# Two token-major sections of 512 columns in a diffusion block, with the attention's values read back from DRAM

## The chip, the cores and the metric

The kernel runs on one core of a Trainium2 chip, all in one launch. The metric is the device time in microseconds (us). The program is built with a tile framework: the source names operations on tiles, and the framework inserts the waits and sets the order in which each engine issues its instructions, following its own estimate of when each is ready. The engines are PE (TensorE, matmuls), DVE (VectorE), ACT (ScalarE), POOL (GpSimd) and SP (SyncE, which issues most DMAs). Each engine works through its own queue in order.

## The reference

One layer of a hybrid backbone is applied to 512 sample tokens and 128 context tokens (640 rows, `T`; the samples are `TS` = 512 of them). What matters here:

```python
proj = h @ lw['w_in']                     # (640, 1024) @ (1024, 3328)
(a_x, a_b, a_c, b_q, b_ff, b_fb, b_i, b_g, c_q, c_k, c_v, d_u, d_v) = split(proj)   # 256 columns each
y_b, s_f, s_b = hgrn2_bidir(b_q, b_ff, b_fb, b_i, b_g, ...)
#   o = o_f + o_b;  o = o * rsqrt(mean(o * o, per head) + EPS);  y_b = o * norm_g * silu(b_g)
y_c = neighbourhood_attention(qh, kh, vh, ctx_k, ctx_v, rpb)    # samples: 8x16 windows on an 8 x 64 grid
#     context_attention(qh, kh, vh)                              # context tokens
y_d = chunk_gmlp(d_u, d_v, ...)            # rmsnorm of d_v over its 256 columns, then a product with d_u
merged = sum of gate_x * (y_x @ w_br_x) over the four branches;  return merged @ w_o
```

The rest (adaLN modulation, a convolutional FFN of 2 x 2816 columns, norms) follows or surrounds it. The context's keys and values are outputs too.

## The kernel before

**Stages.** A boot stage normalizes the input and makes its transposed copy, split into a high and a low part in a rounded 32-bit type (`xh`, `xl`), as every weight is. A product of two such operands is three matmuls: high x high, low activation x high weight, high activation x low weight. Then come the 13 sections of `w_in`, the gates and branches, `w_o`, and the FFN.

**Units.** The work is a list of units, each with a load, a preparation (`wsplit`: ACT makes the high part, DVE the low one) and a compute step. Loads are issued up to four units ahead, preparations two ahead; raw weights have three buffers, prepared ones three. Sections are listed in `SECTIONS` (L57): ff, fb, q, i, g, dv, du, ck, cq, cv, ac, ax, ab, with two units each. For the sections in `LOWD` (ac, ax, ab, and gate d) the low part is made by a DMA that adds into its target, issued from POOL.

**Two layouts.** Most sections are feature-major (`in_tile`, L904): a 128 x 128 block of the weight is stationary, 320 tokens move, twice per block, and the result has features on partitions. The sections i and dv are token-major (`tok_tile`, L917): a block of `xh` or `xl` with 128 tokens is stationary, 256 weight columns move, and the result has tokens on partitions. Such a section holds five PSUM banks over its two units: both `g` buffers (two banks each) and one of the four `m` banks. ACT empties them (L939) at its end.

**Jobs beside it.** HGRN (`hgrn`, from L448), gMLP (`gmlp`), the short convolution, the attention (`attn`) and the adaLN columns (`ada_cols`) are Python generators. `tick` adds the estimated PE time of each step of a unit, and runs a job's next piece when its due time has come. So small matmuls of the jobs stand between the large ones of the units. A dictionary `R` tells one job of another's progress.

**HGRN's end** (L614 to L658). Once the gate is there (`g_done`), five token tiles of the output are made in PSUM; ACT copies them to `og` (L631) and squares them (L632), DVE reduces and scales (L611). Then each tile is transposed (L649) and multiplied by the gate, which is feature-major like the result (L653). The whole is split into high and low parts (`split_y`, L663 and L664) and stored to DRAM (`ybd`).

**Attention's values.** cv is feature-major in region G. The attention needs its values token-major, in seven windows of 128 tokens (two rows of blocks of 8 x 8 grid cells) in `vw`, and the context's values in `vpt`. It makes them by PE transposes of `cv` (L750, L763), copied out of PSUM by DVE (L754, L765). The first reader of `vpt` is the context attention (L800), that of `vw` the first piece of the window attention (L866).

**Regions.** Large buffers are shared by name (`region`): the next tile of a region waits until the last reader of the one before is done.

## Time and profile before

| | us |
|---|---|
| median of 3 runs | 1022.59 (1022.56 to 1022.63) |
| span of the profiled execution | 1020.8 |
| PE busy in the span | 1008.7 (99%) |
| DVE busy | 789.7 (77%) |
| ACT busy | 538.4 (53%) |
| POOL busy | 106.1 (10%) |

The profiled execution's own time is its span, 1020.8 us, and some 1.8 us around it make up the time of a run. The touched part lies between about 64 and 285 us of the span. In rows of the timeline the columns are start, duration (both us), engine, line, operation, output<-inputs, shape and count; what ended the engine's idle time before stands in brackets. A row with a count merges neighbours of the same kind. Groups of instructions read: line, engine, operation, tiles, shape, count | busy us, mean ns of one | idle time before. Matmuls overlap in the records, so a matmul's duration is longer than the time until the next one starts.

### The profile page before, as it was taken

Reading aid. Unit: us, or ns where it says so; the run is one execution under the profiler, and the core shown is the slowest. Engines: PE = TensorE matmul, PEld = TensorE weight load, DVE = VectorE, ACT = ScalarE, POOL = GpSimd, SP = SyncE. Lnnn points to the kernel's source line nnn. Section 1 sums busy time; section 2 is a strip of 40 time slices with the busy share of each in tenths; the row PEclk is TensorE's granted clock in tenths of the full one; section 3 lists DMA queues with packets and bytes.
Section 4 is the critical chain, followed back from the end, with each engine's and each line's share of the span. In section 5 each row is a group of like instructions: output and inputs, shape, how many; then the busy total and the mean of one; then the engine's idle time right before and its main releaser. Section 6 shows DMA issues by size and latency. Waiting matters only on the chain.

```text
span 1020.8 us, 18766 instructions
## 1 busy us (share of the span) xinstructions
PE 1008.7 (99%) x7572; PEld 953.0 (93%) x7572; DVE 789.7 (77%) x1308; ACT 538.4 (53%) x933; POOL 106.1 (10%) x153
## 2 busy tenths in 40 slices
PE   8999999999999999999999999999999999999997
PEld 6899999999999999999998899999999999888886
DVE  6759899779857676776868879988888887797644
ACT  6642343354545454444544567777777776633432
POOL 1000020322100000000010111111122211001101
PEclk9999999999999999999999999999999999999999
DMA  9864333697562413323288585755555669974212
GB/s 355 322 217 130 126 117 116 168 284 226 120 207 79 155 58 104 136 66 104 61 283 337 212 325 121 198 151 150 150 151 151 157 161 274 363 249 157 83 42 103
DMA packets 55926, 177.85 MB, mean 174 GB/s; under 512 B 8192, under 2 KB 14624, under 8 KB 53280
## 3 DMA queue, kind: packets, MB, share of 16 engines
q1 hardware_dynamic: 45008, 140.60, 40.2%
q0 software_dynamic: 10832, 36.06, 14.7%
q8 instruction: 59, 0.97, 0.4%
q14 instruction: 27, 0.22, 0.1%
HBM read 134.93 MB, written 25.46 MB: 157 GB/s over the span
## 4 chain that ended last, share of the span: by engine, by line
PE 92%; DVE 4%; DMA 2%; ACT 1%; issue 1%; SPq 0%; POOLq 0%; POOL 0%; DVEq 0%; ACTq 0%
PE g L1480 20%; PE m L1124 17%; PE g L363 14%; PE g L1815 8%; PE m L1815 6%; PE g L1137 5%; PE m L1480 4%; PE m L1264 3%; PE g L935 2%; PE g L1264 2%; PE m L149 2%; PE g L149 1%; PE m L1475 1%; PE m L527 1%; DMA A<-in_w_ada_dram 1%
## 5 line engine op out<-in xcount | busy, mean ns | idle before, releaser
L363 PE MATMUL g<-XH,w 128*128 128x320 f32 x704 | 171.0, 317 | 0.1
L363 PEld LDWEIGHTS g<-XH,w 128*128 128x128 f32 x704 | 120.6, 188 | 2.5 <-issue 1.0
L363 PE MATMUL g<-XL,w 128*128 128x320 f32 x352 | 108.7, 309 | 0.0
L363 PEld LDWEIGHTS g<-XL,w 128*128 128x128 f32 x352 | 66.3, 188 | 0.1
L312 DVE TENSOR_TENSOR w<-raw,w 128x1024 fp32r<-128x1024 f32 x34 | 41.5, 1221 | 14.7 <-ACT w L311 9.0
L1124 PE MATMUL m<-XH,w 128*128 128x320 f32 x224 | 52.5, 309 | 0.0
L1815 PE MATMUL g<-w,XH 128*128 128x512 f32 (+1 forms) x216 | 50.2, 385 | 0.0
L1815 PEld LDWEIGHTS g<-w,XH 128*128 128x128 f32 x216 | 39.5, 188 | 8.3 <-ACT XH L1774 0.3
L311 ACT ACTIVATE w<-raw 128x1024 fp32r<-128x1024 f32 x34 | 35.7, 1049 | 21.4 <-PE g L1264 9.9
L1815 PE MATMUL g<-w,XL 128*128 128x512 f32 (+1 forms) x180 | 42.5, 387 | 0.0
L149 DVE SCALAR_TENSOR_TENSOR X<-MG,p2t,X 128x641 f32<-128x641 f32 x44 | 38.9, 884 | 4.3 <-ACT X L149 3.4
L149 DVE SCALAR_TENSOR_TENSOR X<-X,p2t,X 128x641 f32<-128x641 f32 x44 | 38.8, 883 | 1.9 <-ACT X L149 1.0
L1815 PEld LDWEIGHTS g<-w,XL 128*128 128x128 f32 x180 | 33.4, 188 | 7.4 <-DVE dt L1830 0.7
L149 ACT ACTIVATE w<-raw 128x1024 fp32r<-128x1024 f32 (+3 forms) x46 | 38.5, 852 | 2.5 <-DMA raw<-in_w_in_dram 1.4
L1480 PE MATMUL g<-XL,w 128*128 128x320 f32 x240 | 38.6, 310 | 0.0
L1480 PE MATMUL g<-XL,C 128*128 128x320 f32 x240 | 38.4, 309 | 0.0
L1124 PEld LDWEIGHTS m<-XH,w 128*128 128x128 f32 x224 | 38.2, 188 | 0.0
L1480 PEld LDWEIGHTS g<-XL,w 128*128 128x128 f32 x240 | 36.0, 188 | 0.5 <-ACT MG L149 0.3
L1815 PE MATMUL m<-w,XH 128*128 128x512 f32 (+1 forms) x156 | 36.4, 381 | 0.0
L1480 PEld LDWEIGHTS g<-XL,C 128*128 128x128 f32 x240 | 36.0, 188 | 0.4 <-ACT MG L149 0.4
L1124 PE MATMUL m<-XL,w 128*128 128x320 f32 x112 | 34.6, 309 | 0.0
L1815 PEld LDWEIGHTS m<-w,XH 128*128 128x128 f32 x156 | 28.5, 188 | 5.6
(549 smaller groups left out, 2749.8 us busy)
## 6 DMA issues: line engine op xcount, KB each, us to landing
raw<-in_w_up_dram SPq DMA_DIRECT2D x30, 512.0 KB, 5.0
raw<-in_w_gp_dram SPq DMA_DIRECT2D x21, 640.0 KB, 3.9
raw<-in_w_down_dram SPq DMA_DIRECT2D x22, 512.0 KB, 4.2
raw<-in_w_in_dram SPq DMA_DIRECT2D x19, 512.0 KB, 4.3
H<-in_w_adt_dram SPq DMA_DIRECT2D x16, 512.0 KB, 4.2
actd<-X POOLq DMA_DIRECT2D x22, 320.5 KB, 5.5
X<-in_w_adt_dram SPq DMA_DIRECT2D x10, 512.0 KB, 4.3
upd<-XL SPq DMA_DIRECT2D x4, 1280.0 KB, 6.5
```

Of the source, the lines that this page charges most:

```text
L149: r = f(*args, **kw)
L311: act(w[0], raw, AF.Copy)
L312: vec.tensor_tensor(w[1], raw, w[0].bitcast(F32), ALU.subtract)
L363: mm(o, w[:, h, k0 + k, :], r(k)[:, s], start=(k == 0 and i == 0), stop=(k == kt - 1 and i == 2))
L527: mm(m[W * g:W * g + W, (i - s0) * W:(i - s0 + 1) * W], lhs, rhs, start=True, stop=True, tile_position=(64 * par, W * g))
L935: mm(o, x(kx)[:, ts], w[:, h, k, :], start=(kx == 0 and i == 0), stop=(kx == 7 and i == 2))
L1124: mm(o, w[:, k, :], x[:, k, :], start=(first and k == 0 and j == 0), stop=(k == 3 and j == 2), skip_group_check=True)
L1137: mm(pb[:, c, 0:HC], w[:, h + k, :], y[:, x, k, s], start=(k == 0 and j == 0), stop=(k == 1 and j == 2))
L1264: mm(m, mh[k // 2][:, hx, k % 2, t * P:(t + 1) * P], wo[q][:, hw, k % 2, :], start=(k == 0 and i == 0), stop=(k == 7 and i == 2))
L1475: mm(o, w[:, k, :], x[:, k, :], start=(first and not part and k == 0 and j == 0), stop=(part == 1 and k == 3), skip_group_check=True)
L1480: z = mm(o, w[:, k, :], x[:, k, :], start=(first and k == 0 and j == 0), stop=(k == 3 and j == 2), skip_group_check=True)
L1815: mm(ps, sl[k][hx][:, t * P:(t + 1) * P], w[:, hw, k, c0:c1], start=first, stop=end and (last or nh == 1 and t == 4 and kk_ == 7))
```

## The change

The four sections i, dv, g and cv become two token-major sections of 512 columns: `iv` holds i and dv, `gc` holds g and cv. Each has four units, each unit two of the eight k blocks with 512 columns. Their weights are packed on the host accordingly; the loads keep their size of 512 KB. The order of the sections changes: du follows iv directly, gc follows du.

The gate is token-major now. HGRN multiplies it in while it takes the output from PSUM, on DVE; after the transposes, ACT and DVE write the high and low parts piece by piece straight from PSUM, and `split_y` is not called there.

The attention's values are token-major too. ACT copies each token tile of cv from PSUM into a small buffer (tag `gt`, shared with other short-lived tiles), and SP stores it to a DRAM tile `cvd`. The attention job loads `vpt` with one DMA and each of the seven windows with two DMAs of 64 partitions. The transposes and their copies are gone, and region G is not used for cv. The attention and `g_operands` start after cq, which has the place that cv had.

```diff
--- before.py
+++ after.py
@@ -54,7 +54,8 @@
 
 OFF = dict(ax=0, ab=256, ac=512, q=768, ff=1024, fb=1280, i=1536, g=1792,
            cq=2048, ck=2304, cv=2560, du=2816, dv=3072)
-SECTIONS = ["ff", "fb", "q", "i", "g", "dv", "du", "ck", "cq", "cv", "ac", "ax", "ab"]
+SECTIONS = ["ff", "fb", "q", "iv", "du", "gc", "ck", "cq", "ac", "ax", "ab"]
+TOK = {"iv": ("i", "dv"), "gc": ("g", "cv")}
 
 
 C_C, C_BADA, C_N1, C_N2 = 0, 16, 64, 72
@@ -405,9 +406,6 @@
         elif sec == "q":
             dd = need("D", "HD", [P, 2560])
             act(c2(dd[:, n * T:(n + 1) * T]), psv, AF.Silu)
-        elif sec == "g":
-            o = need("MG1", "HO", [P, 2560])
-            act(c2(o[:, 1280 + n * T:1280 + (n + 1) * T]), psv, AF.Silu)
         elif sec == "du":
             x0 = need("X0", "DX0", [P, 2560])
             act(c2(x0[:, n * T:(n + 1) * T]), psv, AF.Copy)
@@ -425,13 +423,10 @@
             if (sec, n) == ("ab", 1):
                 drain(lambda: "ada39" in R)
                 R["ya"] = split_y("A", y[:, 1].rearrange("p n t -> p (n t)"))
-        elif sec in ("ck", "cq", "cv"):
-            if sec == "cv":
-                dst = need("G", "CG", [P, 1280])[:, n * T:(n + 1) * T]
-            else:
-                f = need("F", "CF", [P, 2560])
-                o = 0 if sec == "ck" else 1280
-                dst = f[:, o + n * T:o + (n + 1) * T]
+        elif sec in ("ck", "cq"):
+            f = need("F", "CF", [P, 2560])
+            o = 0 if sec == "ck" else 1280
+            dst = f[:, o + n * T:o + (n + 1) * T]
             sc = 0.125 if sec == "cq" else 1.0
             cg, cw = (4, 16) if sec == "cq" else (8, 8)
             dv = dst[:, 0:TS].rearrange("p (g r c) -> p r g c", g=cg, r=8)
@@ -441,6 +436,7 @@
             act(dst[:, TS:T], ps[:, 1, 192:320], AF.Copy, scale=sc)
 
 
+    cvd = dram.tile([T, 256], F32, name="cvd")
     ybd, ycd = [dram.tile([P, 2, 2, T], F32, name=n) for n in ("ybd", "ycd")]
 
 
@@ -628,8 +624,9 @@
                        vt[:, t * 256 + h * 64:t * 256 + (h + 1) * 64],
                        start=(t == 4), stop=(t == 4 or par == 1), skip_group_check=True)
                     pe(0.21)
-            act(og[:, t * 256:(t + 1) * 256], m[:, 0:256], AF.Copy)
-            act(o2[:, t * 256:(t + 1) * 256], m[:, 0:256], AF.Square)
+            tb = slice(t * 256, (t + 1) * 256)
+            act(o2[:, tb], m[:, 0:256], AF.Square)
+            vec.tensor_tensor(og[:, tb], m[:, 0:256], sg[:, tb], ALU.mult)
             yield 0.5
 
             s4 = ss[:, 4 * t:4 * t + 4]
@@ -643,17 +640,19 @@
         normed(last)
         R["hgrn_y"] = True
         yield HY
+        w = region("D", [P, 2, 2, T], F32R)
         for t in range(5):
             m = pm()
             for pr in range(2):
                 ten.transpose(m[:, pr * P:(pr + 1) * P],
                                     og[:, t * 256 + pr * P:t * 256 + (pr + 1) * P], ident)
                 pe(0.11)
-                s = sg[:, pr * T + t * P:pr * T + (t + 1) * P]
-                vec.scalar_tensor_tensor(s, m[:, pr * P:(pr + 1) * P],
-                                         p1[:, C_HN + pr:C_HN + pr + 1], s, ALU.mult, ALU.mult)
+                h, l = [w[:, x, pr, t * P:(t + 1) * P] for x in range(2)]
+                mo, gn = m[:, pr * P:(pr + 1) * P], p1[:, C_HN + pr:C_HN + pr + 1]
+                act(h, mo, AF.Copy, scale=gn)
+                vec.scalar_tensor_tensor(l, mo, gn, h.bitcast(F32), ALU.mult, ALU.subtract)
             yield 0.4
-        nc.sync.dma_start(ybd, split_y("D", sg).bitcast(F32))
+        nc.sync.dma_start(ybd, w.bitcast(F32))
         R["hgrn_done"] = True
         R["yd"] = split_y("E", R["yt"])
 
@@ -717,7 +716,6 @@
         while "yd" not in R:
             yield 1
         ck, cq = R["CF"][:, 0:1280], R["CF"][:, 1280:2560]
-        cv = R["CG"]
         x0 = region("X0", [P, 2560])
         x1 = region("X1", [P, 2560])
         bm = region("B", [P, 2560])
@@ -742,27 +740,16 @@
         pool.memset(btt[:, :, 256:384], 0.0)
 
         offs = [0, 2, 4, 6, 1, 3, 5]
-        for g in range(0, 7, 2):
-            grp = offs[g:g + 2]
-            m = pm()
-            for j, o in enumerate(grp):
-                for pr in range(2):
-                    ten.transpose(m[:, (j * 2 + pr) * P:(j * 2 + pr + 1) * P],
-                                        cv[:, pr * T + o * 64:pr * T + o * 64 + P], ident)
-                pe(0.22)
-            n_ = len(grp) * 256
-            vec.tensor_copy(vw[:, g * 256:g * 256 + n_], m[:, 0:n_])
-            yield 0.4
+        nc.sync.dma_start(vpt, cvd[TS:T])
+        cvw = cvd[0:TS].rearrange("(r g c) v -> r g c v", r=8, c=8)
+        for i, o in enumerate(offs):
+            for g in range(2):
+                nc.sync.dma_start(vw[64 * g:64 * g + 64, i * 256:(i + 1) * 256], cvw[:, o + g])
         m = pm()
         for pr in range(2):
             ten.transpose(m[:, pr * P:(pr + 1) * P], ck[:, pr * T + TS:(pr + 1) * T], ident)
             pe(0.11)
         vec.tensor_copy(ktk, m[:, 0:256])
-        m = pm()
-        for pr in range(2):
-            ten.transpose(m[:, pr * P:(pr + 1) * P], cv[:, pr * T + TS:(pr + 1) * T], ident)
-            pe(0.11)
-        vec.tensor_copy(vpt, m[:, 0:256])
         R["cg"] = True
         nc.sync.dma_start(o_cv[0, 0].rearrange("h s d -> s h d"), vpt.rearrange("p (h d) -> p h d", h=4))
         yield 0.4
@@ -898,8 +885,8 @@
     def plain(ld, cp):
         units.append((ld, lambda pr: pr(), cp))
 
-    SLACK = {"q": 1.3, "du": 1.4, "ax": 1.0, "cv": 1.1}
-    starts = {"q": hgrn, "du": gmlp, "ax": conva, "cv": attn}
+    SLACK = {"q": 1.3, "du": 1.4, "ax": 1.0, "cq": 1.1}
+    starts = {"q": hgrn, "du": gmlp, "ax": conva, "cq": attn}
 
     def in_tile(sec, n, w):
         ps = pg()
@@ -909,49 +896,55 @@
             R[sec + "_done"] = True
         if n == 1 and sec in starts:
             start(starts[sec](), 1.5, SLACK[sec])
-            if sec == "cv":
+            if sec == "cq":
                 start(g_operands())
             if sec == "q":
                 start(ada_cols(range(16, 40), "S0", col_home, HD[4], 10), HD[7])
 
-    def tok_tile(sec, kh, w):
-
-        if kh == 0:
+    def tok_tile(sec, kq, w):
+
+        if kq == 0:
             g0, g1 = pg(), pg()
-            R[sec + "_ps"] = [g0[:, 0, :], g0[:, 1, :], g1[:, 0, :], g1[:, 1, :], pm()]
-            if sec == "i":
-                dst = need("E", "HE", [P, 2560])[:, 1280:2560]
+            R["tok_ps"] = [g0[:, 0, :], g0[:, 1, :], g1[:, 0, :], g1[:, 1, :], pm()]
+            if sec == "iv":
+                need("E", "HE", [P, 2560])
+                R["DX1"] = region("X1", [P, 2560])
             else:
-                dst = region("X1", [P, 2560])
-                R["DX1"] = dst
-            R[sec + "_dst"] = dst
-        dst = R[sec + "_dst"]
+                need("MG1", "HO", [P, 2560])
         for t in range(5):
-            o = R[sec + "_ps"][t][:, 0:256]
-            for k in range(4):
-                ts = slice(t * P, (t + 1) * P)
-                kx = kh * 4 + k
+            o = R["tok_ps"][t]
+            ts = slice(t * P, (t + 1) * P)
+            for k in range(2):
+                kx = kq * 2 + k
                 for i, (x, h) in enumerate(((xhk, 0), (xlk, 0), (xhk, 1))):
                     mm(o, x(kx)[:, ts], w[:, h, k, :], start=(kx == 0 and i == 0), stop=(kx == 7 and i == 2))
-                tick(0.33)
-            if kh == 1:
-                v = dst[:, t * 256:(t + 1) * 256]
-                act(v, o, AF.Copy)
-                if sec == "dv":
-                    act(dst[:, 1280 + t * 256:1280 + (t + 1) * 256], v, AF.Square,
-                        accum_out=dss[:, t:t + 1])
-        if kh == 1:
-            R[sec + "_done"] = True
-
-    TOK = ["i", "dv"]
+                tick(0.68)
+            if kq < 3:
+                continue
+            cs = slice(t * 256, (t + 1) * 256)
+            if sec == "iv":
+                vi, dv = R["HE"][:, 1280:2560], R["DX1"]
+                act(vi[:, cs], o[:, 0:256], AF.Copy)
+                act(dv[:, cs], o[:, 256:512], AF.Copy)
+                act(dv[:, 1280 + t * 256:1280 + (t + 1) * 256], dv[:, cs], AF.Square, accum_out=dss[:, t:t + 1])
+            else:
+                act(R["HO"][:, 1280 + t * 256:1280 + (t + 1) * 256], o[:, 0:256], AF.Silu)
+                c = gp.tile([P, 256], F32, tag="gt", name=nm("cv"))
+                act(c, o[:, 256:512], AF.Copy)
+                nc.sync.dma_start(cvd[ts], c)
+        if kq == 3:
+            R["i_done" if sec == "iv" else "g_done"] = True
+
     for s in SECTIONS:
+        if s in TOK:
+            i = list(TOK).index(s)
+            for kq in range(4):
+                plain(lambda i=i, kq=kq: rows(a["w_tok"][i, kq], 2, 512),
+                      lambda w, s=s, kq=kq: tok_tile(s, kq, w))
+            continue
         for n in range(2):
-            if s in TOK:
-                plain(lambda s=s, n=n: rows(a["w_tok"][TOK.index(s), n], 4, 256),
-                      lambda w, s=s, n=n: tok_tile(s, n, w))
-            else:
-                plain(lambda s=s, n=n: feat(a["w_in"][OFF[s] // P + n], dma=s in LOWD),
-                      lambda w, s=s, n=n: in_tile(s, n, w))
+            plain(lambda s=s, n=n: feat(a["w_in"][OFF[s] // P + n], dma=s in LOWD),
+                  lambda w, s=s, n=n: in_tile(s, n, w))
 
     hdr = dram.tile([2, 2, P, 4, HC], F32, name="hdr")
 
@@ -2139,8 +2132,8 @@
 
     w_in = f("w_in")[0]
     arr["w_in"] = tiles(w_in, 8, P)
-    arr["w_tok"] = np.stack([tiles(w_in[:, OFF[s]:OFF[s] + 256], 8, 256)[0].reshape(P, 2, 4, 256)
-                             .transpose(1, 0, 2, 3) for s in ("i", "dv")])
+    w = [np.concatenate([w_in[:, OFF[s]:OFF[s] + 256] for s in x], 1) for x in TOK.values()]
+    arr["w_tok"] = np.stack([tiles(x, 8, 512)[0].reshape(P, 4, 2, 512).transpose(1, 0, 2, 3) for x in w])
     br = np.concatenate([f("w_br_" + b)[0] for b in "abcd"], 1)
     arr["w_gate"] = tiles(np.concatenate([f("w_gate")[0], br], 0), 10, P)
 
```

## The prediction

> **What bounds the kernel now.** I read the page first (span, busy shares, the chain that ended last), then the sums by stage, then TensorE's instructions in order of time.
>
> ```profile
> span 1020.8 us, 18766 instructions
> PE 1008.7 (99%) x7572; PEld 953.0 (93%) x7572; DVE 789.7 (77%) x1308; ACT 538.4 (53%) x933; POOL 106.1 (10%) x153
> ...
> PE 92%; DVE 4%; DMA 2%; ACT 1%; issue 1%; SPq 0%; POOLq 0%; POOL 0%; DVEq 0%; ACTq 0%
> ```
>
> TensorE (PE) is busy 99% of the span and carries 92% of the chain. "Busy" can hide slow matmuls, so the stage that the change touches is looked at by itself.
>
> ```profile
> 0.00:50.00 50.00, 46.07 (x528) 38.57 (x529) 32.66 (x98) 32.38 (x58) 3.31 (x10) 1.00 0.91 344
> ...
> 100.00:150.00 50.00, 49.90 (x1093) 47.31 (x1091) 43.30 (x77) 20.30 (x39) 5.60 (x6) 1.00 0.38 126
> 150.00:200.00 50.00, 50.00 (x448) 47.99 (x447) 43.10 (x105) 20.15 (x49) 7.22 (x7) 1.00 0.44 125
> ...
> 900.00:1020.00 120.00, 113.89 (x518) 94.19 (x517) 74.67 (x110) 42.18 (x66) 10.49 (x10) 0.99 0.35 119
> ```
>
> Columns: stretch, length, then busy us of PE, weight loads, DVE, ACT, POOL, then granted clock, DMA share, GB/s. Between 100 and 200 us PE idles 0.10 us; most of its idle time (3.9 and 6.1 us) lies in the first and last stretch, which the change leaves alone. The clock is 1.00. So what PE no longer has to do there is time saved, as long as no new wait appears. What a matmul really costs is the spacing of starts, read from unbroken stretches:
>
> ```profile
> 70.75 0.28 PE L935 MATMUL g<-w,XL 128*128 128x256 f32 x1
> ...
> 74.35 0.28 PE L935 MATMUL g<-w,XL 128*128 128x256 f32 x1
> ...
> 307.66 1.92 PE L363 MATMUL g<-E,w 128*128 128x320 f32 x12
> 309.42 0.31 PE L1124 MATMUL m<-XH,w 128*128 128x320 f32 x1
> ...
> 532.57 3.79 PE L1264 MATMUL g<-w,E 128*128 128x512 f32 x16
> ```
>
> Between the first two rows lie 30 starts: 3.60/30 = 0.120 us for 256 columns. Twelve of 320 columns take 1.92 us, the last one alone 0.31: 1.61/11 = 0.1465. Sixteen of 512 columns: (3.79 - 0.39)/15 = 0.2267. All three are N/2.4 ns plus about 13 ns: each matmul has a fixed part, whatever its width.
>
> **The change, part by part.**
>
> *Sections.* Removed: i and dv, each 5 token tiles x 8 k x 3 products = 120 matmuls of 256 columns, and g and cv, each 2 tiles x 2 halves x 8 x 3 = 96 of 320. That is 240 x 0.120 + 192 x 0.1465 = 28.8 + 28.1 = 56.9 us. Added: 2 sections x 120 = 240 of 512 columns (the type and stationary size are those of L1264): 240 x 0.2267 = 54.4 us. Gain 2.5 us, all on PE. Columns are equal (122,880 both ways); the gain is 192 fixed parts.
>
> *Transposes.* The attention no longer turns cv: 14 on L750 and 2 on L763 go.
>
> ```profile
> 208.19 0.60 PE L750 MATMUL m<-cst,G 128*128 128x128 f32 x4
> 208.54 0.39 PE L363 MATMUL g<-XH,w 128*128 128x320 f32 x1
> 208.77 0.30 PE L363 MATMUL g<-XL,w 128*128 128x320 f32 x1
> ```
>
> Four of them hold the stream from 208.19 to 208.54, and the next matmul takes 0.23 us instead of 0.147: 0.35 + 0.083 = 0.433, or 0.108 each. Sixteen: 1.7 us, also on PE. The ten transposes of the HGRN output stay.
>
> *ACT and DVE.* Neither sets the end here, so these are costed at nothing, with PE's matmuls as the cover.
>
> ```profile
> 114.54 0.38 ACT L939 ACTIVATE X<-g 128x256 f32<-128x256 f32 x1 [1.34 <-PE g L935]
> 114.96 0.42 ACT L941 ACTIVATE X<-X 128x256 f32<-128x256 f32 x1
> 115.28 0.19 ACT L941 ACTIVATION_READ_ACCUMULATOR X<-X 128x1 f32 x1
> ...
> 204.89 1.27 ACT L663 ACTIVATE D<-MG 128x1280 fp32r<-128x1280 f32 x1 [3.87 <-DVE MG L653]
> 206.63 0.66 ACT L440 ACTIVATE G<-g 128x320 f32<-128x320 f32 x2 [0.46 <-PE g L363]
> ...
> 208.82 0.69 DVE L754 COPY X<-m 128x512 f32<-128x512 f32 x1 [1.13 <-PE m L750]
> ...
> L872 ACT ACTIVATE C<-m 128x128 fp32r<-128x128 f32 x8 | 2.2, 273 | 9.1 <-PE m L866 9.1
> L611 DVE TENSOR_TENSOR MG<-MG,hss 128x256 f32<-128x256 f32 x5 | 2.1, 425 | 4.3 <-POOL hss L306 4.3
> ```
>
> iv empties its PSUM in its last unit: per token tile two copies (0.38 each) and a square with its accumulator (0.42 + 0.19), 1.4 us of ACT against 6 x 0.2267 = 1.36 us of PE. So ACT runs full for about 7 us and ends 1 to 2 us late. The next unit, du, takes the pair of banks that was emptied first, and has 6.8 us before it needs the second pair; without that cover the price would be those 1 to 2 us. gc needs a Silu and a copy, about 0.8 us per tile, which fits. In the HGRN tail the ACT copy of each output tile becomes a DVE product with the gate (5 x 0.43 = 2.1 us), the split (1.27 on ACT and one pass of DVE) becomes ten small ACT pieces (10 x 0.27 = 2.7 us) with DVE pieces of the old shape behind them. The attention loses its DVE copies (3 x 0.69 and two smaller). DVE sheds some 2 us, ACT stays about level; between nothing gained and the 2 us of DVE gained I take nothing, since PE idles only 0.10 us there.
>
> *The order.* Units stay 26; "du" comes two units earlier, the gate values are complete at the end of the sixteenth unit instead of the tenth. Who waits for them is the HGRN output loop, which polls for g.
>
> ```profile
> 163.81 0.44 ACT L440 ACTIVATE F<-g 128x320 f32<-128x320 f32 x1 [5.15 <-PE g L363]
> ...
> 179.45 1.00 PE L627 MATMUL m<-E,MG 128*128 128x64 f32 x8
> ```
>
> 163.81 is the eviction of the sixteenth unit of before (ck, second tile); the output loop starts at 179.45. Less the 2.5 us, the gate is ready 18 us early. Cost nothing; if the loop came 18 us sooner it would wait.
>
> *The values by way of DRAM.* SP issues five stores of 128 KB, one load of 128 KB (context values) and fourteen of 64 KB (windows), and the store of the context values to the output now waits for a landing, not for a DVE copy.
>
> ```profile
> 59.96 2.05 SPq L676 DMA_DIRECT2D G<-in_gmlp_b_dram  x2
> ...
> 142.36 0.70 ACT L413 ACTIVATE X<-g 128x640 f32<-128x640 f32 x1
> ...
> 163.87 1.22 DVE L263 SCALAR_TENSOR_TENSOR X<-X,S 128x1024 f32<-128x1024 f32 x1
> ...
> 194.17 0.42 SPq L737 DMA_DIRECT2D B<-in_cache_v_dram  x1
> 197.65 0.34 SPq L739 DMA_DIRECT2D X<-in_amask_dram  x1
> ...
> 201.03 8.16 SPq L317 DMA_DIRECT2D raw<-in_w_in_dram  x2
> ...
> B<-in_cache_v_dram SPq DMA_DIRECT2D x1, 128.0 KB, 3.8
> ...
> 221.26 0.66 PE L800 MATMUL m<-B,X 128*64 128x128 f32 x8
> ```
>
> Issue: about 0.4 us each, 20 x 0.4 = 8 us of SP spread over 60 us. Behind them on SP stand the weight loads and the columns of the adaLN weights. SP stands waiting 8.16 us at 201.03 anyway. The rows also show that loads go out when their buffer is free and not where the program names them: gmlp's biases at 59.96 belong to a job that starts after du's last eviction (142.36), the attention's cached values at 194.17 to one that starts after cv's (206.63). The window blocks go to X0, which the adaLN columns are the last to leave, at 165.1; the context values go to X1, free when the mask is loaded (197.65), so they land at about 198.5 + 3.8 = 202. Their first reader is L800, at 221.26 in before, some 217 after. Cost nothing, with 15 us of cover; the other end of the bound is the slower rival below.
>
> *Sum.* 2.5 + 1.7 = 4.2 us. The profiled span 1020.8 becomes 1016.6. The runs' median, 1022.59, is 1.8 us above that span, so 1018.4 us.
>
> **The rivals.**
>
> *Columns alone (no change).* If the wide matmul pays in this stage what two of 256 pay, 0.240, the new sections cost 57.6 us, 0.7 more than the old; with the transposes the gain is 1.0: 1021.6. For it: equal columns. Against it: 0.2267 on L1264. [...] Chance 4%.
>
> *Contended low halves (no change).* The low halves of the weights from ac on are made by accumulating DMAs, prefetched tightly.
>
> ```profile
> 195.72 1.06 POOL L149 DMA_DIRECT2D w<-raw  x1
> ...
> w<-raw POOLq DMA_DIRECT2D x5, 512.0 KB, 8.1
> ...
> 160.00:170.00 10.00, 10.00 (x75) 9.98 (x74) 9.09 (x21) 2.98 (x8) 0.00 (x0) 1.00 0.31 91
> ...
> 200.00:210.00 10.00, 10.00 (x73) 9.63 (x72) 6.04 (x16) 5.65 (x9) 2.61 (x4) 1.00 0.86 244
> 210.00:220.00 10.00, 10.00 (x74) 9.67 (x73) 8.51 (x19) 4.85 (x13) 0.79 (x2) 1.00 0.98 312
> ```
>
> The half of ac's first tile is issued at 195.72 and lands within 8.1 us, by 203.8; PE wants it at 206.4 (cv's last eviction), 2.5 us earlier after the change: 203.9. If the fourteen window blocks (0.9 MB, 2.9 to 3.8 us at 312 to 244 GB/s) fall into 196 to 204 rather than near 165, where the DMA share is 0.31, PE stalls up to 3.7 us: 1022.1. The same size covers the other small waits: three m banks instead of four for the HGRN levels during gc, and ten ACT pieces ahead of DVE in the tail. Chance 11%.
>
> *Values late (slower).* One mechanism: the context load sits behind a blocked head of SP, and PE stops at L800, since its queue is in order. Behind the wait at 201.03 it would go out at 209.2 and land, at the 8.6 us that stores of 128 KB take in the crowded stretch, at 217.8: no loss yet. Behind the next group it is lost:
>
> ```profile
> 220.56 0.37 SPq L1021 DMA_DIRECT2D D<-hdr  x1
> ...
> out_dram<-X SPq DMA_DIRECT2D x2, 128.0 KB, 8.6
> ```
>
> 220.9 + 8.6 = 229.5 against 217: a stall of 12 us, 1030.9. It decides from a landing past 217 + 4.2 = 221. For it: SP's waits of 8 us. Against: buffers free early, loads that overtake. Chance 20%, other stalls of the moved jobs with it (gmlp now shares DVE, already 8.7 of 10 busy, with the HGRN levels).
>
> **How the numbers follow.** 0.2% is 2.05 us, about what a measurement of this kernel can tell from no change. Forecast 65% (1016.4 to 1020.5: the low end if the 2 us of DVE are gained after all, the high end if half of the gain goes to small waits): faster. No change 4 + 11 = 15%. Slower 20%. The range runs from 1016.4 to 1024.6, where "slower" begins; it leaves out the slower case.
>
> **What would show it.** L935's successor: 240 matmuls of 512 columns with starts 0.227 apart. No transposes from G or of cv. PE idle still about 0.1 us per 50 us from 100 to 250. The ac section starting 2.5 us sooner, the next stage (L1124) 4.2 us sooner, at 305.2 instead of 309.4, and the end by the same. Window blocks issued before 195 us. Wrong: gaps of over 1 us before L800, before the first matmul of ac, or in the levels (L527), or an SP wait in front of the context load.

## The result, and the profile after

The change makes the kernel slower by some 0.3%: 1025.28 us (1024.08 to 1028.84, ten runs) against 1022.60 (1022.25 to 1023.01, ten runs), a ratio of 1.0031 with an interval of [1.0020, 1.0041]. The forecast was 1018.4. The profiled execution took 1024.98 us. Page of the changed kernel:

```profile
span 1023.1 us, 18396 instructions
PE 1007.3 (98%) x7364; PEld 939.0 (92%) x7364; DVE 787.6 (77%) x1307; ACT 537.6 (53%) x939; POOL 107.6 (11%) x153
...
PE 84%; issue 7%; DMA 4%; DVE 3%; ACT 1%; POOL 0%; SPq 0%; POOLq 0%; DVEq 0%; ACTq 0%
```

PE has 208 matmuls and 1.4 us of busy time less, yet the span is 2.3 us longer: PE now stands. The chain of waits holds 84% PE instead of 92, and 7% "issue", time in which an engine waited for nothing that the profile shows. Sums by stage (columns as in the prediction), then PE's starts:

```profile
100.00:150.00 50.00, 47.59 (x1017) 39.01 (x1016) 43.94 (x84) 18.12 (x38) 7.25 (x6) 0.97 0.40 120
150.00:200.00 50.00, 49.84 (x393) 45.71 (x392) 42.92 (x103) 19.36 (x44) 7.28 (x7) 1.00 0.50 154
200.00:250.00 50.00, 48.20 (x362) 44.29 (x361) 37.08 (x90) 26.07 (x61) 11.54 (x15) 1.00 0.95 269
```

```profile
74.42 0.39 PE L920 MATMUL g<-w,XL 128*128 128x512 f32 x1
...
76.68 0.61 PE L920 MATMUL m<-w,XH 128*128 128x512 f32 x2
...
219.24 0.66 PE L787 MATMUL m<-B,X 128*64 128x128 f32 x8
...
312.30 0.31 PE L1117 MATMUL m<-XH,w 128*128 128x320 f32 x1
```

Between the first two rows lie 10 starts: 0.226 us for 512 columns, as forecast. The context attention (L787, before L800) starts 2.0 us sooner. The next stage (L1117, before L1124 at 309.42) starts 2.9 us later. In between, PE idles 2.4 us in the first stretch, with the clock at 0.97, 0.2 in the second and 1.8 in the third; before it was 0.10 from 100 to 200. The view of PE's waits (who waited for whom, us in total, times, longest), the changed kernel:

```profile
PE m L523 <- issue: 1.5, 1, 1.5
...
PE m L647 <- DVE D L653: 1.0, 1, 1.0
PE m L523 <- DVE C L542: 0.9, 1, 0.9
...
PE m L836 <- DVE C L860: 0.4, 1, 0.4
...
PE m L853 <- DVE B L1926: 0.2, 1, 0.2
PE m L853 <- ACT B L1924: 0.2, 1, 0.2
```

The kernel before has one wait in these stages, 0.4 us on L849. L523 are the HGRN levels, pairs of groups of 80 small matmuls, L647 the transposes of HGRN's output, L836 and L853 the attention. Two of the three largest stand together, and the clock falls behind them (timeline, then stretches with the granted clock):

```profile
124.25 0.88 PE L523 MATMUL m<-C,D 64*32 64x32 f32 x80 [0.91 <-DVE C L542]
...
125.95 0.44 PE L523 MATMUL m<-C,D 64*32 64x32 f32 x26
127.89 0.66 PE L523 MATMUL m<-C,D 64*32 64x32 f32 x54 [1.50 <-issue]
```

```profile
125.68:129.09 3.41, 1.91 (x85) 1.39 (x84) 3.41 (x8) 0.00 (x0) 0.00 (x0) 1.00 0.65 173
129.10:132.51 3.41, 3.41 (x10) 2.64 (x9) 3.41 (x7) 0.68 (x1) 0.00 (x0) 0.50 0.75 222
```

For 3.41 us the clock is 0.50: 512 columns take 0.43 us (two starts from 130.28 to 131.13 us), which costs 1.7 us. The bill: waits of 1.5 + 1.0 + 0.9 + 0.8 = 4.2, less 0.4 that the kernel before has too, plus 1.7 of clock is 5.5. Against that stands the gain. PE's busy time is 1.4 us less although the slow clock put 1.7 into it, so the work shrank by 3.1 us and not by the 4.2 of the sum. 5.5 less 3.1 is 2.4, and the span grew by 2.3.

### The profile page after: what moved, and what is told of

It reads as the page before. It is cut to its first block, busy times and chain, and to the rows that moved or that the text cites. A ratio compares the mean times of both kernels' runs of the same rounds, so it can differ in the third digit from the quotient of the medians.

```text
span 1023.1 us, 18396 instructions
## 1 busy us (share of the span) xinstructions
PE 1007.3 (98%) x7364; PEld 939.0 (92%) x7364; DVE 787.6 (77%) x1307; ACT 537.6 (53%) x939; POOL 107.6 (11%) x153
## 4 chain that ended last, share of the span: by engine, by line
PE 84%; issue 7%; DMA 4%; DVE 3%; ACT 1%; POOL 0%; SPq 0%; POOLq 0%; DVEq 0%; ACTq 0%
PE g L1473 19%; PE m L1117 17%; PE g L364 9%; PE g L1808 8%; PE m L1808 6%; PE g L1130 5%; PE m L1473 4%; PE m L1257 3%; PE g L920 2%; PE g L1257 2%; PE m L1468 1%; DMA hdr<-MG 1%; PE m L150 1%; DMA A<-in_w_ada_dram 1%; PE m L523 1%
## 5 line engine op out<-in xcount | busy, mean ns | idle before, releaser
L364 PE MATMUL g<-XH,w 128*128 128x320 f32 x576 | 137.8, 316 | 0.0
L364 PEld LDWEIGHTS g<-XH,w 128*128 128x128 f32 x576 | 98.3, 188 | 1.8 <-issue 0.5
L364 PE MATMUL g<-XL,w 128*128 128x320 f32 x288 | 89.0, 309 | 0.0
L313 DVE TENSOR_TENSOR w<-raw,w 128x1024 fp32r<-128x1024 f32 x38 | 46.4, 1220 | 18.9 <-ACT w L312 18.4
L312 ACT ACTIVATE w<-raw 128x1024 fp32r<-128x1024 f32 x38 | 39.9, 1051 | 29.1 <-PE g L1257 10.1
L364 PEld LDWEIGHTS g<-XL,w 128*128 128x128 f32 x288 | 54.2, 188 | 0.0
L1117 PE MATMUL m<-XH,w 128*128 128x320 f32 x224 | 52.5, 309 | 0.0
L920 PE MATMUL g<-w,XH 128*128 128x512 f32 x128 | 48.5, 422 | 0.0
L1473 PE MATMUL g<-XL,w 128*128 128x320 f32 x240 | 38.6, 310 | 0.0
L1117 PEld LDWEIGHTS m<-XH,w 128*128 128x128 f32 x224 | 38.2, 188 | 0.0
L1473 PEld LDWEIGHTS g<-XL,w 128*128 128x128 f32 x240 | 36.0, 188 | 0.5 <-ACT MG L150 0.3
L1117 PE MATMUL m<-XL,w 128*128 128x320 f32 x112 | 34.6, 309 | 0.0
```

Of the source, the lines that this page charges most:

```text
L312: act(w[0], raw, AF.Copy)
L313: vec.tensor_tensor(w[1], raw, w[0].bitcast(F32), ALU.subtract)
L364: mm(o, w[:, h, k0 + k, :], r(k)[:, s], start=(k == 0 and i == 0), stop=(k == kt - 1 and i == 2))
L920: mm(o, x(kx)[:, ts], w[:, h, k, :], start=(kx == 0 and i == 0), stop=(kx == 7 and i == 2))
L1117: mm(o, w[:, k, :], x[:, k, :], start=(first and k == 0 and j == 0), stop=(k == 3 and j == 2), skip_group_check=True)
L1473: z = mm(o, w[:, k, :], x[:, k, :], start=(first and k == 0 and j == 0), stop=(k == 3 and j == 2), skip_group_check=True)
```

## The experiments

Theories: D, DVE is late for the levels; I, a block of instructions reaches PE late inside a dense group; Q, the order of DVE's queue at HGRN's end and in the attention; later S, PE's program reaches the levels too early for DVE. Other letters (A, B, C, G, L, M) are explained in the expectation that uses them. All medians are of 4 to 12 runs; the runs of the kernel before beside them had medians of 1022.6 to 1022.9, and the ratios with their intervals are taken over the runs, not from the medians. Waits of PE are from one profiled execution each, in us: at the level pairs on DVE, inside a level group on "issue", at HGRN's transposes, and in the attention (L836 and L853 and their successors); then DVE's longest wait in the attention for the load of an adaLN column, and the stretches of halved clock between the first and the last 20 us. Left out are waits of 0.7 to 0.9 us in e5, e6, e9, e10 and e12 for a PSUM bank that ACT empties into a buffer of tag `gt`, 2.0 us in e12 for a prepared weight, and gaps on "issue" among the section matmuls (0.3 to 0.6 us in e1, e6, e8 and e10). The profiled execution is not always near the median: it was the fastest one of e3, e4, e10 and e14, and the slowest of e12.

| kernel | median (range), us | ratio to before | levels | issue | transposes | attention | column load | clock, us |
|---|---|---|---|---|---|---|---|---|
| before | 1022.60 | 1 | 0 | 0 | 0 | 0.4 | 0 | 0 |
| changed | 1025.28 (1024.1-1028.8) | 1.0031 [1.0020, 1.0041] | 0.9 | 1.5 | 1.0 | 0.8 | 2.2 | 3.4 |
| e1_shift | 1028.27 (1025.1-1028.8) | 1.0047 [1.0035, 1.0059] | 1.9 | 0 | 1.1 | 3.5 | 5.5 | 6.8 |
| e2_gmlp | 1028.86 (1023.1-1030.2) | 1.0049 [1.0035, 1.0064] | 0.9 | 1.8 | 0 | 4.9 | 7.0 | 6.8 |
| e3_iv | 1030.85 (1030.5-1032.0) | 1.0082 [1.0069, 1.0095] | 0.4 | 2.1 | 1.6 | 2.0 | 2.2 | 3.4 |
| e4_high_dve | 1030.80 (1027.5-1031.1) | 1.0072 [1.0060, 1.0084] | 0.6 | 1.2 | 1.5 | 3.6 | 5.0 | 3.4 |
| e5_yields | 1027.67 (1025.8-1028.5) | 1.0044 [1.0032, 1.0056] | 0.9 | 1.8 | 2.1 | 0.2 | 0 | 3.4 |
| e6_both | 1026.03 (1024.5-1027.4) | 1.0030 [1.0019, 1.0041] | 1.7 | 0 | 2.1 | 0.2 | 0 | 3.4 |
| e7_gc | 1024.60 (1021.9-1028.8) | 1.0017 [1.0007, 1.0028] | 0 | 1.2 | 0.3 | 0.9 | 2.3 | 0 |
| e8_levels | 1023.37 (1022.1-1028.7) | 1.0010 [0.9999, 1.0020] | 1.9 | 0 | 0 | 1.9 | 3.6 | 3.4 |
| e9_tail | 1028.68 (1026.6-1029.2) | 1.0049 [1.0037, 1.0062] | 0.9 | 1.5 | 0 | 1.7 | 4.0 | 3.4 |
| e10_all | 1024.21 (1022.7-1028.5) | 1.0021 [1.0010, 1.0032] | 1.6 | 0 | 0.8 | 0.2 | 0.4 | 0 |
| e11_spaced | 1024.13 (1022.2-1026.4) | 1.0014 [1.0005, 1.0022] | 0 | 2.1 | 0 | 0.5 | 0 | 3.4 |
| e12_best | 1033.09 (1030.9-1037.9) | 1.0097 [1.0079, 1.0115] | 0 | 1.7 | 0 | 8.4 | 9.9 | 17.1 |
| e13_sp28 | 1022.61 (1021.7-1029.2) | 1.0006 [0.9994, 1.0018] | 0 | 0 | 0 | 0.6 | 0.3 | 0 |
| e14_sp56 | 1025.06 (1021.7-1029.6) | 1.0022 [1.0005, 1.0038] | 0 | 1.2 | 0 | 0.6 | 0 | 0 |
| e15_sp80 | 1022.23 (1020.7-1024.0) | 0.9994 [0.9986, 1.0003] | 0 | 0 | 0 | 0.6 | 0 | 0 |
| e16_before_shift | 1024.92 (1023.5-1025.8) | 1.0017 [1.0009, 1.0026] | 0 | 1.1 | 0 | 0.3 | 0 | 3.4 |
| e17_apart | 1028.37 (1027.5-1029.6) | 1.0056 [1.0044, 1.0068] | 1.5 | 0.8 | 0 | 5.2 | 7.3 | 6.8 |
| e18_apart80 | 1027.81 (1024.6-1029.8) | 1.0048 [1.0034, 1.0063] | 2.0 | 0.3 | 0 | 3.7 | 5.7 | 3.4 |

**The two sections apart.** e3 has only `iv`, in the kernel before; e7 has only `gc`, in the changed kernel, with i and dv as two sections of 256.

```diff
 e3: -SECTIONS = ["ff", "fb", "q", "i", "g", "dv", "du", "ck", ...
     +SECTIONS = ["ff", "fb", "q", "iv", "g", "du", "ck", ...
 e7: -SECTIONS = ["ff", "fb", "q", "iv", "du", "gc", ...
     +SECTIONS = ["ff", "fb", "q", "i", "dv", "du", "gc", ...
```

> The kernel before with only the input gate and the mixer half in one section of 512 columns; gate, attention values, HGRN tail and attention as before, gMLP after the fourteenth unit as before. 120 matmuls of 512 columns in place of 240 of 256: 28.8 - 27.2 = 1.6 us less on TensorE. If the moved jobs around the gate and the values are what costs (theories D and I), this part keeps its gain: 1021.0. If the wide section brings its own stalls (its evictions crowd ScalarE for 7 us), 1022.6 or above.

> The changed kernel with only the section of output gate and attention values in 512 columns; input gate and mixer half as two sections of 256, as before. TensorE's gain: 192 x 0.1465 - 120 x 0.2267 = 0.9 us, and 1.7 us for the sixteen transposes; together 1022.6 - 2.6 = 1020.0 if no stall comes with it. TensorE's stream has its 120 matmuls of 256 columns more again ahead of the levels, so theory I expects the fetch to meet the level groups at another place, without the gap and the halved clock; theory D expects the levels to wait as in the changed kernel, since gMLP and the levels still share VectorE. Theory Q: the attention's stall of about 1 us stays. I and Q: 1021.0 within 1; D: 1024 or more.

e3 misses its first branch by 10 us: the part that looked harmless costs most. It falls under the second (1022.6 or above), but not for the reason given there, since no wait on the section's evictions is in its trace. It has the gap, the halved clock and waits at the levels, the transposes and the attention. e7 has the gap too, which theory I did not expect, without a halved clock, and no wait at the levels; its fastest run (1021.9) is under the kernel before, its slowest 6 us above. So both parts lose time, and their traces show the losses not in the wide sections but in what stands on PE behind them.

**The place of the instructions.**

```diff
-    warm_up(WARM)
+    for i in range(WARM - 56):
+        mm(wps[0:64, 0, 0:152], warm, warm[:, 0:1].to_broadcast([P, 152]), start=True, stop=True)
```

> The changed kernel with 56 of its first 100 warm-up matmuls left out and the other 44 made wider (152 columns), so that the warm-up is as long and everything behind it stands 112 instructions earlier in TensorE's instruction stream; no work is changed. Theory I (instruction fetch): the gap of 1.50 us inside the second group of 80 level matmuls at 126 us (1.2 to 2.1 us at the same place in the three kernels run so far) belongs to a block of instructions that arrived late, and the clock that is halved for 3.41 us right behind it follows from the gap. Then the gap goes, the clock stays at 1.0, and the time falls by 1.5 to 3.3 us from 1025.3, to 1022.0 to 1023.8. Theory D (VectorE late): the gap is a wait for a result of VectorE that the trace names badly; then nothing moves, 1025.3 within 0.6.

Half right. Timeline of PE with the shift:

```profile
124.05 0.88 PE L524 MATMUL m<-C,D 64*32 64x32 f32 x80 [0.71 <-DVE C L543]
...
125.76 0.89 PE L524 MATMUL m<-C,D 64*32 64x32 f32 x80
...
133.56 0.88 PE L524 MATMUL m<-C,E 64*32 64x32 f32 x80 [1.16 <-DVE C L543]
```

The second group runs through: the gap was no wait for data. What is left of it, 0.56 us on "issue", stands behind the group at 127.88 us, among section matmuls. The clock stayed at 1.0 there. But the time did not fall: the next pair now waits 1.16 us for DVE, which the gap had covered, and the attention stalls 3.5 us with a halved clock behind it. The gap hid a wait.

**gMLP.** Its start goes back to the fourteenth unit, and then both edits go together (e8). (In the expectation below, the changed kernel starts gMLP at the end of du, the twelfth unit.)

```diff
-    starts = {"q": hgrn, "du": gmlp, "ax": conva, "cq": attn}
+    starts = {"q": hgrn, "ax": conva, "cq": attn}
 ...
+        if (sec, kq) == ("gc", 1):
+            start(gmlp(), 1.5, SLACK["du"])
```

> The changed kernel with the gMLP job started after the fourteenth unit, where the kernel before had it, instead of after the eighth of its units' list end at du (the twelfth). Theory D (VectorE is full when the levels need it): the wait of 0.91 us on VectorE at 123 us goes, VectorE's busy share between 110 and 120 us falls from 9.8 to about 8.5 of 10, and the time falls by 0.9 us (the wait alone, 1024.4) to 4.2 us (with the gap of 1.50 and the clock that fell behind it, 1021.1). Theory I (instruction fetch by itself): the wait goes, but the gap of 1.5 us stays where it is, since no instruction of TensorE ahead of it moves; 1024.4. Theory L (gMLP must be early, the tail of HGRN waits for it): slower than 1025.3.

> The changed kernel with two of the edits together: TensorE's instructions 112 earlier (as in the shift alone) and gMLP started after the fourteenth unit (as in the kernel before). Each alone left the stretch of the level groups long: 43.4 us from the first to the last pair with the shift, 44.8 with the later gMLP, 44.6 in the changed kernel, 42.0 before. Theory B (two causes that cover one another: the late block of instructions, and the 3.6 us of gMLP on a VectorE that is full there): with both gone the stretch is 42 to 42.5 us, with no halved clock at 129 us, 2.3 us less than the changed kernel there and 1.7 us for the clock; what the attention then does is as in the changed kernel or the two edits alone (1 to 4 us of stalls). Theory S (the levels are late because the wide matmuls bring TensorE to each level sooner than VectorE's chain of about 8 us for a level allows, whatever gMLP does): the stretch stays at 43.4 or more.

With gMLP's start moved back the wait is still 0.9 us and the gap 1.8, and with both edits the levels wait 1.9 us in all, so theory B's forecast fails. But the edit moves only a part of gMLP. Its ten later pieces (L691, from 137 us on in the changed kernel) are gone from the levels. Its first five products, which scale dv (L681), stand on DVE at 109.9 us in e2 and 109.7 in e8, hardly sooner than in the changed kernel (110.2): where the job starts in the source does not decide where they stand in DVE's queue. So these runs clear the later pieces and not the first ones. e2 is slower, as theory L says, but in the attention, by a late column, and not in HGRN's tail. Theory S was put up next.

**The spacing of the levels.** What stands between the first and the last level pair, by line (stretch, length, busy us with overlaps and count, clock, DMA share, GB/s); the kernel before (L935 of 256 columns, L363 of 320), the changed one (L920 of 512, L364) and e11 (the same two):

```profile
110.61:152.60 41.99, 9.16 (x64) 1.00 0.35 114
110.61:152.60 41.99, 24.20 (x150) 1.00 0.35 114
```

```profile
107.91:152.53 44.62, 21.28 (x75) 0.96 0.40 122
107.91:152.53 44.62, 10.36 (x64) 0.96 0.40 122
```

```profile
109.46:157.76 48.30, 26.43 (x99) 0.96 0.40 128
109.46:157.76 48.30, 9.51 (x55) 0.96 0.40 128
```

At the spacings of the prediction that is 64 x 0.120 + 150 x 0.1465 = 29.7 us of section matmuls before, 75 x 0.2267 + 64 x 0.1465 = 26.4 after, 30.5 in e11. Over the same stretches DVE is busy 38.63 of 41.99 us before and 41.78 of 44.62 after. PE's program puts 3.3 us less between the pairs, and DVE is busy 92% and 94% of the time.

```profile
110.61:152.60 41.99, 41.89 (x1032) 38.56 (x1031) 38.63 (x70) 19.68 (x40) 5.60 (x6) 1.00 0.35 114
```

```profile
107.91:152.53 44.62, 42.21 (x980) 33.77 (x979) 41.78 (x79) 13.44 (x21) 7.25 (x6) 0.96 0.40 122
```

That sum does not explain the waits. Counted the same way, e2 and e8 have 29.8 us of section matmuls in the stretch and DVE busy for 39.1 and 39.0 us, much like the kernel before, and still wait; e7 has the 26.4 us of the changed kernel and does not wait. DVE's rows tell more. The kernel before (DVE, then PE at the third pair), then DVE in the changed kernel:

```profile
111.55 0.51 DVE L532 COPY_PREDICATED D<-lmask,m 128x320 f32<-128x320 uint8 x1 [2.21 <-PE m L527]
...
122.74 1.55 DVE L546 TENSOR_TENSOR C<-C,A 128x640 f32<-128x640 f32 x2
```

```profile
126.89 0.89 PE L527 MATMUL m<-C,D 64*32 64x32 f32 x80
```

```profile
110.22 0.35 DVE L681 TENSOR_SCALAR X<-X,dss 128x256 f32<-128x256 f32 x1 [1.06 <-POOL dss L307]
...
110.62 0.51 DVE L528 COPY_PREDICATED D<-lmask,m 128x320 f32<-128x320 uint8 x1
111.02 1.13 DVE L681 TENSOR_SCALAR X<-X,dss 128x256 f32<-128x256 f32 x4
...
122.56 1.55 DVE L542 TENSOR_TENSOR C<-C,A 128x640 f32<-128x640 f32 x2
```

The third pair reads the products that DVE writes into C. Before, DVE stands ready for the first pair's results and has these products 13.7 us after the first pair starts (110.61 to 124.29); PE comes to the third pair after 16.3 us, 2.6 us later than DVE. In the changed kernel gMLP's first products are in the way. DVE stands 1.06 us for POOL, then makes the five products (1.5 us), with the first level's results in between. So it needs 16.2 us (107.91 to 124.11), and PE, which comes after 15.4 (124.25 less the wait of 0.91), waits. In the kernel before the five products stand behind the third pair, from 135.0 us on.

DVE's 2.5 us are thus gMLP's, and PE's coming 0.8 us sooner adds to them. In the other kernels DVE needs 13.7 us in e16, where these products come later, 15.3 in e7, where part of the delay lies ahead of the first pair and PE needs 15.45, 17.4 in e12, and 16.2 or 16.3 in all the rest. No run moves the five products alone. That the waits would go with them is worked out from the rows and not tried: at 13.7 us DVE would be 1.7 us ahead of PE. HD[1] is the planner's step behind each level; a larger one lets PE come later:

```diff
-HD = [4, 5, 2.1, 7, 2.2, 1.4, 1.5, 5, 2.0, 2, 11]
+HD = [4, 5.8, 2.1, 7, 2.2, 1.4, 1.5, 5, 2.0, 2, 11]
```

> The changed kernel with one number changed: the planner's step behind each level, HD[1], is 5.8 for 5, so that some 0.8 to 1.4 us more of section matmuls stand on TensorE between two pairs of level groups. Theory S (VectorE is full between 108 and 152 us and needs about 42 us for the five steps between pairs; the changed kernel puts only 26.3 us of section matmuls between them where the kernel before had 29.6, and TensorE waits for the rest): the waits at the pairs (0.9 and up to 1.5 us) shrink below 0.5 us, the dense groups stand at other places of the instruction stream, and unless the fetch hits one again the clock stays at 1.0; 1025.3 - 1.5 to 4 = 1021 to 1024, less clear if the attention stalls by 3 us as in other variants. Theory G (gMLP on VectorE is the cause): nothing changes but the place of the waits, 1025 or more.

The waits for DVE are gone from the levels and from the transposes, with gMLP where the change put it, as S forecast: PE now comes to the third pair 21.2 us after the first, and DVE still needs 16.2. This is a cure and does not decide the cause, since more time for DVE covers gMLP's products too. A gap of 2.1 us stays, six matmuls before the end of a group:

```profile
119.99 0.84 PE L523 MATMUL m<-C,E 64*32 64x32 f32 x74
122.95 0.33 PE L523 MATMUL m<-C,E 64*32 64x32 f32 x6 [2.12 <-issue]
```

**The place of the instructions again**, on e11 with three shifts (edit as in e1, with 28, 56 and 80 for 56), and on the kernel before.

> The changed kernel with HD[1] 5.8, and TensorE's instructions 56 earlier (28 warm-up matmuls fewer, the rest 92 columns wide). Theory I (the gap hangs on where the blocks of instructions fall): the gap of 2.3 us at 120.6 us of the kernel with HD[1] 5.8 moves by 28 matmuls inside its group or leaves it; without gap and halved clock 1024.1 - 2.3 - 1.7 = 1020.1, with them 1024. Rival (the gap belongs to the group, whatever the place): 1024.

> The same with 112 instructions earlier (56 warm-up matmuls fewer, the rest 152 columns wide). Theory I: the boundary moves past the end of the group that had the gap; unless another group is hit, no gap and no halved clock: 1020.1. Rival: 1024.

> The same with 160 instructions earlier (80 warm-up matmuls fewer, the rest 340 columns wide). Theory I: as with 112; 1020.1 without a gap, 1022 to 1024 if another dense group is hit. Rival: 1024 at the same place.

> The kernel before with the shift of 112 instructions and nothing else. If its blocks only stood in a good place: a gap of 1 to 2 us inside a level group and a halved clock, 1024.5 to 1026. If the change itself brings the gap (TensorE reaches the groups sooner, or the DMA engines are busier then): no gap, 1022.6 within 0.6.

With 28 and 80 no gap stands inside a group, the clock stays up, and the medians are 1022.61 and 1022.23; with 56 another group is hit (1.2 us) and the runs scatter (1021.7 to 1029.6). The trace with that gap is of the fastest run, so the gap alone cost little there; what its longer runs did, no trace shows. The forecast of 1020.1 is met by none of the medians; e13 and e15 are level with the kernel before, their intervals take in 1. Two smaller waits are left there, 0.7 us for an `m` bank of gMLP and 0.5 for ScalarE's eviction of du. The kernel before with nothing but the shift:

```profile
128.42 0.82 PE L528 MATMUL m<-C,D 64*32 64x32 f32 x73
130.37 0.33 PE L528 MATMUL m<-C,D 64*32 64x32 f32 x7 [1.13 <-issue]
```

It loses 2.3 us (1024.92), with the clock halved behind the gap. So the kernel before has its instructions in a good place, as far as one shift can tell, and the change moves them: section `iv` alone has 120 matmuls and their weight loads less.

**The attention and HGRN's end.** DVE and SP of the changed kernel (timeline):

```profile
201.51 1.22 DVE L264 SCALAR_TENSOR_TENSOR junk<-A,S 128x1024 bf16<-128x1024 f32 x1
...
212.79 0.42 DVE L752 COPY X<-m 128x256 f32<-128x256 f32 x1 [4.31 <-PE m L750]
...
217.21 1.22 DVE L264 SCALAR_TENSOR_TENSOR A<-A,S 128x1024 f32<-128x1024 f32 x1
...
228.11 1.22 DVE L264 SCALAR_TENSOR_TENSOR junk<-A,S 128x1024 bf16<-128x1024 f32 x1 [2.18 <-DMA A<-in_w_adt_dram]
...
230.53 1.01 DVE L823 TENSOR_TENSOR X<-m,B 128x384 f32<-128x384 f32 x2
```

```profile
222.03 0.43 SPq L250 DMA_DIRECT2D A<-in_w_adt_dram  x1
```

```profile
214.58 0.83 SPq L249 DMA_DIRECT2D A<-in_w_adt_dram  x1
```

An adaLN column in buffer A has its first product at 201.5 us and its second at 217.2, behind the pieces of HGRN and of the context attention, for which DVE stands 4.31 us. So A's next load goes out at 222.0 (in the kernel before at 214.6, the last row), DVE waits for it, and the softmax (L823) stands behind the column in DVE's queue.

```diff
 e5: @@ attn, behind the window loads
+        for i in range(4):
+            yield 0.4
 e4: @@ hgrn
-                act(h, mo, AF.Copy, scale=gn)
+                vec.tensor_scalar(h, mo, gn, None, ALU.mult)
 e6: e5 and e1   e9: e5 and HY = 8 for 5
 e10: e1, e2, e5, and the pause of ada_cols begins at "hgrn_out" instead of "hgrn_y"
 e12: e10, HD[1] 5.8 for 5 and HY 6.5 for 5
```

> The changed kernel with the ten high pieces of the HGRN output made by VectorE (multiply by the norm's column, round) instead of ScalarE. Theory A (the low piece stands on VectorE behind a high piece that stands on ScalarE behind other evictions, and TensorE waits 1.05 us at 201.7 us for the bank): the wait goes and the time falls by about 1.0 us, to 1024.2. Theory C (VectorE is the one that is short there): ten more pieces of about 0.25 us on VectorE, the wait stays or grows, 1025.3 to 1027.

> The changed kernel with four steps of 0.4 put back into the attention's job, where the kernel before had them behind its window transposes. That moves no work, but puts the second product of the adaLN column in buffer A on VectorE ahead of the pieces of the HGRN output and of the context attention; in the changed kernel it stands behind them (first product at 201.5 us, second at 217.2). Theory Q (the order of VectorE's queue): buffer A comes free some 13 us sooner, its next load goes out before 215 us instead of at 222.0, VectorE no longer stands 2.2 to 7 us for that load at 226 to 231 us, and the stalls of TensorE between 225 and 245 us (1.0 us in the changed kernel, 3 to 5 in the variants) go: 1 us less, 1024.3 within 0.6. Theory M (the DMA engines are simply full from 200 to 230 us, the load lands late whenever it is issued): the wait of VectorE stays, 1025.3 or more.

> Both edits together, the shift of TensorE's instructions and the four steps in the attention. Theories I and Q: their gains add, 1025.3 - 1.5 to 3.3 - 1.0 = 1021.0 to 1022.8. If the one only moves a stall to the other's place, it is no better than the better of the two.

> The changed kernel with the four steps of 0.4 back in the attention and the HGRN output's transposes three steps later (HY 8 for 5). With the four steps alone, the stalls at 225 to 245 us went, but TensorE waited 2.3 us for the bank of its third output tile at 202.4 us, since two adaLN products (2.4 us) now stood ahead of VectorE's first low piece. Theory Q: when the transposes come some 2 to 3 us later, that wait goes (under 0.5 us), and what is left against the kernel before is the levels' 2.6 us and the halved clock: 1023 to 1025. If the wait only moves with the transposes: 1025 to 1028.

> The changed kernel with four edits: the shift of TensorE's instructions, gMLP after the fourteenth unit, the four steps in the attention, and the adaLN columns stopped from the end of the HGRN output loop on, a few us sooner than now (so that no product of theirs stands ahead of the low pieces). No work is changed. If the three places (levels, output transposes, attention's softmax behind a late column) are all that eats the gain of 4.2 us, the time is 1018.4 to 1020.5, under both kernels. If not, a stall has only moved: 1022 or more, and the trace names its place.

> All edits of the kernel with four edits, and two numbers more: HD[1] 5.8 for 5 (levels further apart on TensorE) and HY 6.5 for 5 (the output's transposes later). Theory S: of the 3.7 us that the four edits left unexplained, the waits at the levels (0.5 and 1.25 us) and at the third output tile (1.1 us) go: 1024.2 - 2.5 = 1021.7, or 1020 in executions without a halved clock, at or under the kernel before. If the waits only move to the attention, 1023 to 1025.

e4 goes as theory C says: the transposes wait 1.5 us instead of 1.0, so taking ScalarE out does not free them. e5 does what Q says: in its trace A's load goes out at 206.5 us, DVE waits for no column, the attention's stalls are 0.2 us; and the two products now delay the transposes by 2.1 us, and the time is worse. e6 adds little; e9 takes the transposes' wait away and gets the attention's back (1.7). e10 is the mildest there, and still waits at the levels. e12, put together from edits that had each taken a wait away, is the worst of all: an 8.4 us wait.

```profile
245.52 1.23 DVE L265 SCALAR_TENSOR_TENSOR junk<-H,S 128x1024 bf16<-128x1024 f32 x1 [9.93 <-DMA H<-in_w_adt_dram]
```

The table shows a regularity in this: where DVE waits 2 us or more for a column's load in the attention, PE waits there 1.4 to 2.3 us less than DVE (3.5 for 5.5, 4.9 for 7.0, 8.4 for 9.9, 1.9 for 3.6), e3 alone excepted; without such a wait it stands 0.2 to 0.6. Why a load lands late in one kernel and not in the next probably hangs on where the framework's order puts the column's two products; it was not settled for each.

**The groups of a pair further apart** (e17, and e18 with the shift of 80).

```diff
-                    yield 3 if l == 4 else 0.4
+                    yield 3 if l == 4 else 2
-HD = [4, 5, 2.1, ...     +HD = [4, 4.4, 2.1, ...
```

> The changed kernel with the two groups of 80 matmuls of a level put further apart: the planner's step between them is 2 for 0.4, and the step behind the level 4.4 for 5, so that the levels take as long together as with HD[1] 5.8. Theory I (too many instructions in too short a time): about nine section matmuls instead of three stand between the groups, the instructions of 320 matmuls last 4 us instead of 2.9, and the gap, the halved clock and the waits at the pairs are smaller than with HD[1] 5.8 alone: 1022 or less, against 1024.1. Rival (the second group now comes too late for VectorE's chain, which lengthens): new waits at the pairs, 1025 or more.

> The same with 160 instructions earlier (80 warm-up matmuls fewer, the rest 340 columns wide). Theory I: no gap at either place of the blocks, so the same time as without the shift within 1 us, 1020 to 1022. Rival: as there, 1025 or more.

The rival holds: the gap shrinks to 0.8 and 0.3 us, but the pairs wait 1.5 and 2.0 us for DVE, and the attention has its late column again. No version beats the kernel before by more than the measurement tells.

## Why the prediction was wrong

- *What bounds the kernel, and the sections.* PE is the bound, and 512 columns cost 0.226 us in an unbroken stretch, as forecast. But the term was too large: added up from each start to the next, without idle time, the matmuls on the sections' lines (L363 and L935 before) take 208.0 us before and 206.4 to 206.5 in e13, e14 and e15, whose clock stays up. That is 1.5 us less, not 2.5. Where the missing 1 us lies was not followed up.
- *Transposes.* They are gone, and nothing took their place on PE. Added up in the same way the sixteen take 1.3 us in the kernel before, where the sum has 1.7.
- *The gain as a whole.* PE is busy 1008.7 us before and 1005.9, 1005.8 and 1006.4 in e13, e14 and e15: 2.3 to 2.9 us less where the sum has 4.2. So some 1.5 us of the error is the gain, and the larger part is what follows.
- *ACT and DVE at nothing*: **the step that failed**, with "PE idles only 0.10 us there" as its cover. A PE that never waits was read as slack of the others. It was the opposite: at the third level pair of the kernel before DVE's products lie ready only 2.6 us before PE comes for them. The change puts gMLP's first products ahead of them, which costs DVE 2.5 us, 1.06 of it standing for POOL, and PE comes 0.8 us sooner: a wait of 0.9 us, and more in the kernels in which no gap hides the next one. Further on PE waits 1.0 us for DVE at the transposes and 0.4 us more than before in the attention. The DVE time shed in the tail (2 us) lies after the levels and could not help. The evictions of iv did fit; du shows no wait in the changed kernel.
- *The order at nothing*: the same mistake. The gate was ready in time, as worked out. But dv is complete sooner, and gMLP's first products with it, ahead of the levels' own. The order also sets where the blocks of instructions fall (a gap of 1.5 us and 1.7 us of slow clock here; e16: 2.3 us for a shift alone), and where the columns stand in DVE's queue. None of the three had a term in the sum.
- *Values by way of DRAM.* Right: the windows go out from 170.4 us on, the context values at 204.4 (6 us later than worked out, behind a weight load on SP), and L787 starts at 219.24 without a wait. What moved was the order of DVE's queue, through the four `yield`s that went with the transposes: with them back (e5) the late column is gone, but the transposes wait and the time is no better.

```profile
170.42 1.98 SPq L747 DMA_DIRECT2D X<-cvd  x3
...
204.44 0.42 SPq L743 DMA_DIRECT2D X<-cvd  x1
```

- *Rivals.* "Columns alone" did not occur (the sections gained 1.5 us and did not lose 0.7), and no wait for a low half shows in the changed kernel; small waits for three `m` banks did show in e15 (0.7 us), and the pieces in the tail made 1.0 us. The slower rival named the wrong place, L800; its half sentence on "gmlp now shares DVE" with the levels named what delays DVE there, without a price. The sign for "wrong" that the prediction gave, gaps of over 1 us in the levels, is what the trace shows. 1025.28 lies 0.7 us above the top of its range.

## What to carry to other kernels

Where one engine is 99% busy beside another that is 92% busy, look up for each hand-over how long the second engine's result lies ready before the first one comes for it (2.6 us here). Whatever an edit puts into the second engine's queue ahead of that, the waiting included, has to fit into this lead, though no wait shows before. Look for it in the engine's rows and not in the source, since a job's pieces need not stand where the job starts. After any edit ahead of a dense stretch of small instructions, look for gaps on "issue" inside it (1.5 us in the changed kernel, 1.1 in e16) and for the clock behind it (0.50 for 3.41 us in both), and try the kernel of before with a harmless shift: the difference of two kernels can be the place of their instructions. A job queued on an engine on whose results the critical one depends is only hidden while its loads land in time (in e12 DVE stands 9.9 us for a column, and PE 8.4).
